# Projections in token order: the residue order made as queries and keys leave PSUM, and for values by a trip through DRAM

## The chip, the cores and the metric

One Trainium2 chip, of which the kernel uses one core. The metric is the device time of one execution in microseconds (us). Five engines matter here: the tensor engine (PE, with its weight loads shown apart as PEld), the vector engine (DVE), the scalar engine (ACT), GpSimd (POOL) and the sync engine (SP), which in this kernel issues every DMA.

## What is computed

The reference is one layer of a decoder trunk on 512 tokens of 1024 channels: a normalisation, one large input projection (`w_in`, 11520 columns), three causal token mixers on slices of it, gates, three branch projections that are merged, and an output projection with a residual. All is float32. Cut to what the change touches:

```python
hn = rms_norm(x, ln_g[l])
proj = jnp.einsum('bsd,dc->bsc', hn, w_in[l])
(qa, ka, va, ga, qb, kb, vb, gb, qc, kc, vc, gc, gate_logits) = jnp.split(proj, ...)
...
DIL_PAIRS = ((128, 1), (512, 4), (2048, 16))      # mixer B: (window, dilation) of three head groups
...
for gi, (w, d) in enumerate(DIL_PAIRS):
    steps = jnp.arange(n_keys[gi]) * d
    idx = t[:, None] + w - steps[None, :]
    k_g = k_pads[gi][:, idx]
    v_g = v_pads[gi][:, idx]
    logits = einsum('bqhd,bqjhd->bhqj', q_c[:, :, gi], k_g) * scale + bias_g[gi][:, None, :]
```

In the groups with dilation 4 and 16 a query sees only keys whose distance is a multiple of 4. Sorted by residue modulo 4, the 512 tokens fall into four tiles of 128, and the queries of a tile have all their keys in the tile of the same residue. That order (residue 0: tokens 0, 4, 8, ..., then residue 1, ...) is called the residue order here.

## The kernel before

Every matrix product is done in three passes, with each float32 operand split in a high and a low part (`whi`, `wlo`, `xhi`, `xlo`; the low part is what the high one leaves over). The normalised hidden state lies transposed in SBUF, as `xhi` and `xlo`, 128 channels by 8 channel tiles by 512 tokens.

The attention work is cut into ten units, in this order: A0, W0, R0, Z0, A1, W1, R1, Z1, C0, C1. The letter is the kind (A is mixer A, W, R and Z are the dilations 1, 4 and 16 of mixer B, C is mixer C), the digit the half of the heads: four heads each. A unit has a projection and an attention:

- Projection (`project`, line 351): for each of four tiles of 128 tokens, 24 matmuls (8 channel tiles by three passes, lines 362 to 364) into one PSUM tile `pj`. The hidden state is the stationary operand (what the weight load brings in, 128 columns), the weight of `w_in` the moving one: 512 columns for queries and keys together, 256 for values. For the units R and Z the stationary operand is `perm_view(xhi[:, k, :], "R")[:, t]`, that is every fourth token: 128 float32 elements that lie 16 bytes apart. For all others it is 128 neighbouring elements.
- Queries and keys leave `pj` by ACT (line 374), are normalised per head (ACT squares, line 376; DVE sums, line 378; POOL takes the power, line 141; DVE multiplies, line 389), are transposed on PE (line 412, the queries reversed within the tile), and are written to SBUF with their gain (units R and Z: ACT, line 415, to `qf` and `kf`). Values leave `pj` by a cast on ACT and a subtraction on DVE (lines 386 and 387, shown as the helpers' lines 130 and 135), to `vhi` and `vlo`.
- Attention of R and Z (`residue_attention`, line 507), for each pair of heads: eight score matmuls (line 522, tile t of queries against tile t of keys), a DVE pass that adds the bias and takes the minimum (436), an exponential on ACT (437), transposes on PE (533), a split of these into `pthi` and `ptlo` (ACT and DVE, 130 and 135), the product with the values (lines 425 to 427, from `mm3`) and an eviction to `oraw` in token order (ACT, line 550). `kf` and `qf` of tile t come from projection tile t alone.

After the unit Z a joint softmax over the three groups follows (lines 711 to 749; its ACT copies `un` stand at line 718). After the units there are the raw gate columns, the gates, the branch products and the output product, all of them runs of matmuls.

Weights of `w_in` are loaded ahead on SP's queue (`load_w`, line 146), into four buffers `w32`, then split by ACT (`whi`, line 130) and DVE or POOL (`wlo`, line 135) into six buffers each. A unit's queries and keys take four of the six, its values two. Line 642 projects queries and keys first, then the values.

The order in which each engine gets its instructions is not the order of the code: the framework schedules the whole program on a timeline of its own, engine by engine, and the queues are then fixed. So PE's queue mixes the attention of one unit with the projection of the next, and each engine works strictly in its queue's order. PSUM has eight banks in four tags of two (`pj`, `tr`, `sc`, `po`).

Of the kernel before, what the change touches and what calls it, by code (L numbers as in the profile page):

```python
# [30 lines left out]
# per unit: steps of the work that fills the tensor engine (the next unit's projections, or raw gate  # L31
# columns) issued before its attention, and their number after each step of the attention
RATION = {"A0": (52, 0.5), "W0": (52, 0.5), "W1": (52, 0.5), "C0": (8, 0.6), "C1": (0, 0.9)}

# kinds of attention: A causal, W window of 128 and itself, C window of 128, R keys 4 apart,
# Z keys 16 apart (as R, three of four masked). Each: length of its row of biases, distance at the
# row's start, distance between neighbours, largest distance.
# [16 lines left out]
# first columns of w_in's parts  # L54
# [37 lines left out]
def perm_view(v, perm):  # L92
    """Last axis of 512 tokens as (tile, ...) in the order of the kind."""
    if perm == "R":
        return v.rearrange("p (i r) -> p r i", r=4)
    return v.rearrange("p (t i) -> p t i", i=128)


def body(tc, x, ln_g, w_in, qk_g, sinks, w_branch, w_out, rel_bias, c_ident, c_onehot, c_mask, c_expand, out):
# [9 lines left out]
    with top:  # L109
# [36 lines left out]
        def load_w(pieces, kts, early=False):  # L146
            """Pieces of one width side by side: source(k0, k1) -> DRAM view [128, k1 - k0, n].
            Returns the high and the low part as functions of the k tile."""
# [29 lines left out]
        def start_x():  # L178
            """Hidden state: normalised, transposed, split."""
# [40 lines left out]
        def start_bias():  # L220
            """Rows of biases by distance, negated, +BIG where the distance is masked; gains, sinks."""
# [39 lines left out]
        def gate_cols(w, c, psum):  # L261
            """psum [128, 512]: columns c .. c+127 of the loaded chunk, on all tokens."""
            whi, wlo = w
            for k in range(KT):
                a = whi(k)[:, c : c + 128]
                T.matmul(psum, a, xhi[:, k, :], start=(k == 0), stop=False)  # L266
                T.matmul(psum, a, xlo[:, k, :], start=False, stop=False)  # L267
                T.matmul(psum, wlo(k)[:, c : c + 128], xhi[:, k, :], start=False, stop=(k == KT - 1))  # L268
                yield
# [37 lines left out]
        with att:  # L307
# [29 lines left out]
            def stack_queries(qn, dst, tsl):  # L337
                """Four heads' queries, each transposed with its high part on rows 0-63 and its low
                part on rows 64-127."""
# [11 lines left out]
            def project(pieces, perm, w, qbuf=None):  # L351
                """Pieces: (type, destination, columns, gain). Types: q, k, v; K and V are the keys
                and values that several query heads share, doubled."""
                whi, wlo = w
                ncol = sum(p[2] for p in pieces)
                for t in range(NT):
                    tsl = slice(t * 128, (t + 1) * 128)
                    pj = ps.tile([128, 512], F32, name="pj", tag="pj")
                    for k in range(KT):
                        xh = perm_view(xhi[:, k, :], perm)[:, t]  # L360
                        xl = perm_view(xlo[:, k, :], perm)[:, t]
                        T.matmul(pj[:, :ncol], xh, whi(k), start=(k == 0), stop=False)  # L362
                        T.matmul(pj[:, :ncol], xh, wlo(k), start=False, stop=False)  # L363
                        T.matmul(pj[:, :ncol], xl, whi(k), start=False, stop=(k == KT - 1))  # L364
                        if k < KT - 1:
                            yield
# [26 lines left out]
                    for ty, dst, m, gc in pieces:  # L393
                        src = pj[:, o : o + m]
                        if ty == "v":
                            split_hi(dst[0][:, t, :m], src)
                            split_lo(dst[1][:, t, :m], src, dst[0][:, t, :m])
# [6 lines left out]
                        else:  # L404
# [9 lines left out]
                            if len(dst) == 1:  # L414
                                A.activation(dst[0][:, :, tsl], tr[:, :npair], AF.Copy, scale=g)
# [23 lines left out]
            def natural_attention(kind, hf, u, stat, oraw):  # L439
                """Queries in token order against the keys from the start (A) or from the tile before."""  # L440
# [66 lines left out]
            def residue_attention(kind, hf, u, stat, oraw):  # L507
                """Tokens in the order of their residues, so that each tile of queries has its keys in
                the tile of the same number."""
                qf, kf, vh, vl = u  # L510
                for p in range(2):
# [6 lines left out]
                    for t in range(NT):  # L518
                        for e in range(2):
                            rows = slice(e * 64, e * 64 + 64)  # L520
                            qs = slice(t * 128, t * 128 + 128)
                            T.matmul(scs[e][:, t], qf[rows, p, qs], kf[rows, p, qs], start=True, stop=True)  # L522
# [30 lines left out]
            def spread(vals, hf, order, use):  # L553
                """vals: for each group [128, NT, 4], factors per (query, head of this half); order:
                the transpose's moving matrix. Calls use(p, g, expanded) with each pair's factors on
                the pair's 128 channels. High and low parts are stacked in one contraction."""
# [40 lines left out]
            def loads(unit, early=False):  # L597
# [10 lines left out]
                return [load_w([win_piece(q + c, 256), win_piece(k + c, 256)], KT, early), load_w([win_piece(v + c, 256)], KT)]  # L608
# [13 lines left out]
            def unit_project(ui, ws):  # L622
                """Queries, keys and values of a unit."""
# [13 lines left out]
                else:  # L637
# [4 lines left out]
                    yield from project([("q", q, 256, gc), ("k", k, 256, gc + 1)], perm, ws[0])  # L642
                    yield from project([("v" if kind in "RZ" else "V", v, 256, 0)], perm, ws[1])
# [6 lines left out]
            for ui, (kind, hf, gi) in enumerate(units):  # L650
# [58 lines left out]
                elif len(bstate["o"]) == 3:  # L709
                    # the groups' maxima and sums to token order, their joint softmax weights  # L710
# [47 lines left out]
        def silu(br):  # L758
            """silu(gate) times the branch, in two parts."""
# [115 lines left out]
```

## Time and profile before

| | |
|---|---|
| median of 3 runs | 892.51 us |
| lowest, highest | 889.96, 894.52 us |
| span of the profiled execution | 891.1 us |
| the profiled execution's own time | not given apart from its span |
| PE busy | 877.7 us (98%), 4295 matmuls |
| PE weight loads busy | 733.4 us (82%) |
| DVE, ACT, POOL busy | 426.1, 413.5, 172.0 us |
| DMA moved | 75.18 MB, mean 84 GB/s |

The busy time of PE is counted from the modelled start to the modelled end of a matmul, and neighbouring matmuls overlap. So 98% doesn't say that PE does all it could: how fast it goes is read from the distance between the starts of two neighbours. The profile's line numbers are those of the kernel above. Where a line is that of a helper (130, 135, 425 to 427), the tile's name says which use it is.

### The profile page before, as it was taken

The numbers are of one execution on the slowest core, as the hardware profiler recorded it, in microseconds if no ns is written. First come the engines' busy times: TensorE is split into PE (matmuls) and PEld (weight loads), VectorE is DVE, ScalarE is ACT, GpSimd is POOL, SyncE is SP. The second block draws the span as 40 slices with busy tenths as digits, with TensorE's granted clock in tenths as the row PEclk, the third lists the DMA queues.
The fourth block names the chain that finished last, engine by engine and source line by source line (L and its number), as shares of the span: only waits on it lengthen the run. The fifth ranks groups of instructions, "written<-read, shape, count | busy, mean of one in ns | idle before, by whom it ended". The sixth has DMA issues, their size and how long they took to land.

```text
span 891.1 us, 11573 instructions
## 1 busy us (share of the span) xinstructions
PE 877.7 (98%) x4295; PEld 733.4 (82%) x4295; DVE 426.1 (48%) x981; ACT 413.5 (46%) x913; POOL 172.0 (19%) x113
## 2 busy tenths in 40 slices
PE   7999999999999999999999999999999999999998
PEld 5888889888978678998899787777888888888886
DVE  6746455344236656434442468554614554322522
ACT  5535553447468546335464585654623432321410
POOL 4333012020112240220210135010402320120100
PEclk9999999999999999999999999999999999999999
DMA  8434113112014221231121132231333232332202
GB/s 264 127 114 133 48 36 97 58 31 76 32 54 119 64 83 55 72 95 37 32 82 47 30 107 58 85 108 48 127 108 96 95 129 84 121 136 75 99 20 95
DMA packets 54077, 75.18 MB, mean 84 GB/s; under 512 B 4451, under 2 KB 36323, under 8 KB 54020
## 3 DMA queue, kind: packets, MB, share of 16 engines
q1 hardware_dynamic: 54020, 74.44, 26.6%
q8 instruction: 34, 0.56, 0.3%
q14 instruction: 23, 0.19, 0.1%
HBM read 70.17 MB, written 4.26 MB: 84 GB/s over the span
## 4 chain that ended last, share of the span: by engine, by line
PE 93%; DVE 2%; ACT 2%; DMA 1%; issue 1%; POOL 0%; SPq 0%; DVEq 0%; POOLq 0%; ACTq 0%
PE pj L362 13%; PE pj L363 13%; PE pj L364 13%; PE pj L266 7%; PE pj L268 7%; PE pj L267 7%; PE acc L834 5%; PE po L499 4%; PE tr L474 3%; PE po L809 3%; PE po L808 3%; PE po L810 2%; PE sc L425 2%; PE sc L522 2%; PE tr L412 1%; PE sc L427 1%
## 5 line engine op out<-in xcount | busy, mean ns | idle before, releaser
L362 PE MATMUL pj<-whi,xhi 128*128 128x512 f32 (+1 forms) x576 | 223.3, 388 | 2.0 <-DVE whi L132 1.4
L363 PE MATMUL pj<-wlo,xhi 128*128 128x512 f32 (+1 forms) x576 | 217.6, 378 | 0.0
L364 PE MATMUL pj<-whi,xlo 128*128 128x512 f32 (+1 forms) x576 | 216.2, 375 | 0.0
L135 DVE TENSOR_TENSOR wlo<-w,whi 128x1024 fp32r<-128x1024 f32 x82 | 110.0, 1351 | 112.9 <-ACT whi L130 112.3
L362 PEld LDWEIGHTS pj<-whi,xhi 128*128 128x128 f32 x576 | 142.5, 247 | 15.8 <-issue 3.0
L363 PEld LDWEIGHTS pj<-wlo,xhi 128*128 128x128 f32 x576 | 143.0, 248 | 10.2 <-issue 1.7
L364 PEld LDWEIGHTS pj<-whi,xlo 128*128 128x128 f32 x576 | 142.7, 248 | 9.0 <-issue 0.5
L130 ACT CAST whi<-w 128x1024 fp32r<-128x1024 f32 x108 | 113.1, 1051 | 62.8 <-PE po L809 31.7
L135 POOL TENSOR_TENSOR wlo<-w,whi 128x1024 fp32r<-128x1024 f32 x28 | 69.0, 2464 | 292.8 <-ACT whi L130 292.8
L141 POOL TENSOR_TENSOR rr<-rv,mhalf 128x8 f32<-128x8 f32 (+2 forms) x40 | 65.7, 1642 | 306.8 <-DVE rv L139 306.6
L266 PE MATMUL pj<-xhi,whi 128*128 128x512 f32 x288 | 114.8, 399 | 0.0
L268 PE MATMUL pj<-xhi,wlo 128*128 128x512 f32 x288 | 113.7, 395 | 0.0
L267 PE MATMUL pj<-xlo,whi 128*128 128x512 f32 x288 | 113.1, 393 | 0.0
L436 DVE CUSTOM_DVE_ANT_0 lg<-sc,bt 128x128 f32<-128x128 f32 (+3 forms) x128 | 42.4, 362 | 79.4 <-PE tr L474 61.6
L268 PEld LDWEIGHTS pj<-xhi,wlo 128*128 128x128 f32 x288 | 54.1, 188 | 11.9 <-issue 0.5
L266 PEld LDWEIGHTS pj<-xhi,whi 128*128 128x128 f32 x288 | 54.3, 188 | 11.6 <-issue 0.2
L267 PEld LDWEIGHTS pj<-xlo,whi 128*128 128x128 f32 x288 | 54.2, 188 | 11.3 <-issue 0.2
L130 ACT CAST pthi<-tr 128x128 fp32r<-128x128 f32 (+3 forms) x112 | 43.7, 400 | 38.6 <-PE tr L474 22.7
L135 DVE TENSOR_TENSOR ptlo<-tr,pthi 128x128 fp32r<-128x128 f32 (+3 forms) x112 | 50.5, 457 | 22.4 <-ACT pthi L130 22.0
L437 ACT ACTIVATE lg<-lg,sm 128x128 f32<-128x128 f32 (+1 forms) x96 | 40.3, 421 | 24.1 <-DVE sm L436 23.8
L378 DVE TENSOR_REDUCE ss<-sq 128x8 f32<-128x512 f32 (+2 forms) x40 | 25.7, 642 | 48.4 <-ACT sq L376 48.1
L800 ACT ACTIVATE gsg<-pj 128x512 f32<-128x512 f32 x24 | 14.3, 596 | 65.9 <-PE pj L268 65.9
(177 smaller groups left out, 1269.4 us busy)
## 6 DMA issues: line engine op xcount, KB each, us to landing
w<-in_w_in SPq DMA_DIRECT2D x54, 512.0 KB, 3.9
w<-in_w_in SPq DMA_DIRECT2D x72, 256.0 KB, 4.2
w<-in_w_branch SPq DMA_DIRECT2D x12, 512.0 KB, 3.2
w<-in_w_out SPq DMA_DIRECT2D x8, 512.0 KB, 4.5
xt<-in_x SPq DMA_DIRECT2D x4, 512.0 KB, 5.4
bt<-scr SPq DMA_DIRECT2D x8, 256.0 KB, 3.6
bt<-scr SPq DMA_DIRECT2D x16, 128.0 KB, 3.3
osp<-oraw SPq DMA_DIRECT2D x4, 512.0 KB, 4.5
```

Of the source, the lines that this page charges most:

```text
L130: A.copy(dst, src)
L135: eng.tensor_tensor(dst, src, hi.bitcast(F32), ALU.subtract)
L141: G.tensor_tensor(r, v, mhalf[:, :n], ALU.pow)
L266: T.matmul(psum, a, xhi[:, k, :], start=(k == 0), stop=False)
L267: T.matmul(psum, a, xlo[:, k, :], start=False, stop=False)
L268: T.matmul(psum, wlo(k)[:, c : c + 128], xhi[:, k, :], start=False, stop=(k == KT - 1))
L362: T.matmul(pj[:, :ncol], xh, whi(k), start=(k == 0), stop=False)
L363: T.matmul(pj[:, :ncol], xh, wlo(k), start=False, stop=False)
L364: T.matmul(pj[:, :ncol], xl, whi(k), start=False, stop=(k == KT - 1))
L436: V.tensor_tensor_reduce(lg, sc, bt, 1.0, init, ALU.add, ALU.min, mcol)
L437: last_exp[0] = A.activation(lg, lg, AF.Exp, bias=mcol, scale=-1.0, accum_out=lcol)
L834: T.matmul(acc[t * 2 + e], part[k // 2][:, k % 2, tsl], wo[q](k)[:, es], start=(k == 0 and q == 0 and part is mhi), stop=(k == KT - 1 and ...
```

## The change

In the projection every unit takes the hidden state in token order. Units R and Z make the residue order afterwards: the copy of queries and keys from PSUM reads its source with a step of four elements and writes 32 neighbours into each of the four residue tiles; values are split into a new tile `vn` (256 high and 256 low columns, in the ring of three buffers `qn`), each token tile is written to a DRAM scratch of 512 rows, and after the fourth two DMAs read it back in residue order into `vhi` and `vlo`. The values of R and Z are now projected before the queries and keys, and their weights are loaded in that order. Because the queries are still reversed in each token tile, the residue tiles of `qf` stand in reverse, and the scores take tile 3 - t of the queries against tile t of the keys.

```diff
@@ def project @@
-                        xh = perm_view(xhi[:, k, :], perm)[:, t]
-                        xl = perm_view(xlo[:, k, :], perm)[:, t]
+                        xh, xl = xhi[:, k, tsl], xlo[:, k, tsl]
...
                         if ty == "v":
-                            split_hi(dst[0][:, t, :m], src)
-                            split_lo(dst[1][:, t, :m], src, dst[0][:, t, :m])
+                            vn = qkv.tile([128, 512], F32R, name="vn", tag="qn", bufs=3)
+                            split_hi(vn[:, :m], src)
+                            split_lo(vn[:, m : 2 * m], src, vn[:, :m])
+                            vscr = dst[2]
+                            nc.sync.dma_start(vscr[tsl, :], vn.bitcast(F32))
+                            if t == NT - 1:
+                                for i in range(2):
+                                    back = vscr[:, i * m : (i + 1) * m].rearrange("(i r) c -> i r c", r=4)
+                                    nc.sync.dma_start(dst[i].bitcast(F32), back)
...
                             if len(dst) == 1:
-                                A.activation(dst[0][:, :, tsl], tr[:, :npair], AF.Copy, scale=g)
+                                src = tr[:, :npair].rearrange("c p (i r) -> c p r i", r=4)
+                                i0 = 32 * t if ty == "k" else 96 - 32 * t
+                                d4 = dst[0].rearrange("c p (r i) -> c p r i", r=4)
+                                A.activation(d4[:, :, :, i0 : i0 + 32], src, AF.Copy, scale=g)
@@ def residue_attention @@
-                            qs = slice(t * 128, t * 128 + 128)
-                            T.matmul(scs[e][:, t], qf[rows, p, qs], kf[rows, p, qs], start=True, stop=True)
+                            qs = slice((3 - t) * 128, (4 - t) * 128)
+                            ks = slice(t * 128, t * 128 + 128)
+                            T.matmul(scs[e][:, t], qf[rows, p, qs], kf[rows, p, ks], start=True, stop=True)
@@ def loads @@
+                if kind in "RZ":
+                    return [load_w(vv, KT), load_w(qk, KT)]
@@ def unit_project @@
+                    if kind in "RZ":
+                        vscr = dp.tile([S, 512], F32, name=f"vscr{ui}")
+                        yield from project([("v", v + (vscr,), 256, 0)], perm, ws[0])
+                        yield from project(pqk, perm, ws[1])
```

The scheduler puts the work of PE and SP in a new order. Three places matter later.

PE's queue before, where the scores of Z0 begin (`sc<-kf,qf`, line 522; the 256-column matmuls in front are the values of Z0, the 512-column ones behind are queries and keys of A1):

```order
L364 MATMUL pj<-whi,xlo 128x256
L522 MATMUL sc<-kf,qf 128x128 x4
L362 MATMUL pj<-whi,xhi 128x512
L363 MATMUL pj<-wlo,xhi 128x512
L364 MATMUL pj<-whi,xlo 128x512
```

So before, all 96 matmuls of A1's queries and keys stand behind the first of these scores.

PE's queue now at the same scores (line 535), the first pair of heads and then the second (line 546 is the transpose of the exponentials; the 256-column matmuls are the values of A1):

```order
L363 MATMUL pj<-whi,xhi 128x512
L364 MATMUL pj<-wlo,xhi 128x512
L535 MATMUL sc<-kf,qf 128x128 x8
L365 MATMUL pj<-whi,xlo 128x512
L363 MATMUL pj<-whi,xhi 128x512
```

```order
L365 MATMUL pj<-whi,xlo 128x256
L546 MATMUL tr<-idr,lg 128x128
L535 MATMUL sc<-kf,qf 128x128 x2
L546 MATMUL tr<-idr,lg 128x128
L535 MATMUL sc<-kf,qf 128x128 x6
L546 MATMUL tr<-idr,lg 128x128 x2
L363 MATMUL pj<-whi,xhi 128x256
```

The scores of Z0 have moved back by 86 of A1's 96 query and key matmuls: 10 of these stand behind them now, then the 96 of A1's values. The same holds of Z1 in front of C0, where 24 query and key matmuls of C0 and the 96 of C1 stand behind the scores.

SP's queue before, around the weights that follow the biases of R0 (`bt`, line 515; `w` is a weight of `w_in`):

```order
L156 DMA w_2271<-in_w_in 128x2x256 x2
L515 DMA bt<-scr 128x128 x5
L156 DMA w_2278<-in_w_in 128x4x256
L156 DMA w_2284<-in_w_in 128x4x256
L156 DMA w_2818<-in_w_in 128x2x256 x2
```

SP's queue now at the same place (`vscr<-vn` writes a tile of Z0's values to DRAM, `vhi<-vscr` and `vlo<-vscr` read all four back):

```order
L401 DMA vscr_1977<-vn 128x512 x2
L156 DMA w_2300<-in_w_in 128x4x256
L401 DMA vscr_1977<-vn 128x512
L156 DMA w_2306<-in_w_in 128x4x256
L405 DMA vhi<-vscr_1977 128x4x256
L526 DMA bt<-scr 128x128 x3
L405 DMA vlo<-vscr_1977 128x4x256
L526 DMA bt<-scr 128x128 x2
L156 DMA w_2840<-in_w_in 128x2x256 x2
```

Six DMAs of values now stand among the biases and the weights of each of the four units R and Z, and those behind a read-back wait on the queue until it may start.

## Rows read from the trace of the kernel before

**Rows 1.** The page's first part: busy time of each engine, its share of the span, instructions.

```profile
PE 877.7 (98%) x4295; PEld 733.4 (82%) x4295; DVE 426.1 (48%) x981; ACT 413.5 (46%) x913; POOL 172.0 (19%) x113
```

**Rows 2.** The page's fourth part: the chain of work that ended last, shares of the span by engine.

```profile
PE 93%; DVE 2%; ACT 2%; DMA 1%; issue 1%; POOL 0%; SPq 0%; DVEq 0%; POOLq 0%; ACTq 0%
```

**Rows 3.** The answer on the tile `pj`: shortest, median and longest weight load in ns, of the unit projections (line 362) and of the raw gate and gate columns (line 266), with first and last start.

```profile
L362 PEld LDWEIGHTS pj<-whi,xhi x576: 186/192/348, 10.7 to 535.1; 128*128 128x128 f32 x192
...
L266 PEld LDWEIGHTS pj<-xhi,whi x288: 186/188/249, 535.5 to 830.0; 128*128 128x128 f32 x144
```

**Rows 4.** The timeline of PE, start and duration in us, in the values of R0, whose stationary operand has the step of four: the first and the last of 11 neighbours, 10 distances.

```profile
148.19 0.40 PE L363 MATMUL pj<-wlo,xhi 128*128 128x256 f32 x1
...
150.54 0.40 PE L364 MATMUL pj<-whi,xlo 128*128 128x256 f32 x1
```

**Rows 5.** The same in the values of A0, whose stationary operand is contiguous: the first and last of 20 neighbours (19 distances), and of a later 21 (20 distances).

```profile
41.75 0.28 PE L362 MATMUL pj<-whi,xhi 128*128 128x256 f32 x1
...
43.91 0.28 PE L363 MATMUL pj<-wlo,xhi 128*128 128x256 f32 x1
...
46.29 0.28 PE L362 MATMUL pj<-whi,xhi 128*128 128x256 f32 x1
...
48.65 0.28 PE L364 MATMUL pj<-whi,xlo 128*128 128x256 f32 x1
```

**Rows 6.** The same for 512 columns: with the step of four in the queries and keys of Z0 (11 neighbours, 10 distances), and contiguous in W0 (15 neighbours, 14 distances).

```profile
168.64 0.40 PE L363 MATMUL pj<-wlo,xhi 128*128 128x512 f32 x1
...
171.02 0.40 PE L364 MATMUL pj<-whi,xlo 128*128 128x512 f32 x1
```

```profile
54.69 0.39 PE L363 MATMUL pj<-wlo,xhi 128*128 128x512 f32 x1
...
57.96 0.39 PE L362 MATMUL pj<-whi,xhi 128*128 128x512 f32 x1
```

**Rows 7.** The timeline of PE where single steps of R0's values alternate with W0's attention.

```profile
166.92 0.28 PE L427 MATMUL sc<-khi,qlo 64*128 64x256 f32 x1
167.12 0.51 PE L362 MATMUL pj<-whi,xhi 128*128 128x256 f32 x1
167.47 0.40 PE L363 MATMUL pj<-wlo,xhi 128*128 128x256 f32 x1
```

**Rows 8.** Windows: busy time of PE, PEld, DVE, ACT and POOL in stretches (instructions in brackets), granted clock, DMA share, GB/s. The first runs from the second scores of Z0 to the end of A1's projection, the second is the same place in the second half (Z1, C0, C1).

```profile
246.00:293.00 47.00, 46.77 (x297) 39.95 (x294) 26.39 (x89) 34.63 (x86) 9.54 (x6) 1.00 0.28 82
...
488.00:536.00 48.00, 46.57 (x298) 39.79 (x295) 28.54 (x106) 35.22 (x92) 10.89 (x7) 1.00 0.24 74
```

**Rows 9.** Groups of ACT instructions in the stretch 246 to 293 us: count, busy us and mean ns of one, then the idle time before them and what ended it.

```profile
L437 ACT ACTIVATE lg<-lg,sm 128x128 f32<-128x128 f32 x16 | 6.2, 389 | 4.4 <-DVE sm L436 4.4
L130 ACT CAST whi<-w 128x1024 fp32r<-128x1024 f32 x6 | 6.1, 1051 | 0.3 <-PE pj L364 0.3
...
L376 ACT ACTIVATE sq<-qn 128x512 f32<-128x512 f32 x4 | 2.5, 634 | 0.1
L374 ACT COPY qn<-pj 128x512 f32<-128x512 f32 x4 | 2.3, 575 | 1.9 <-PE pj L364 1.9
L130 ACT CAST pthi<-tr 128x512 fp32r<-128x512 f32 x4 | 2.1, 589 | 2.6 <-PE tr L533 2.6
```

**Rows 10.** The chain of waits in order of time, start and duration, at the end of Z0's attention.

```profile
269.72 0.24 PE pj L363
271.29 0.62 ACT oraw L550
...
285.73 0.27 ACT vlo L130
286.03 0.30 DVE vlo L135
286.37 0.38 PE pj L362
...
290.10 0.59 PE tr L412 x4
```

**Rows 11.** Groups of the whole run, different shapes apart: what a weight's low part and the copies cost.

```profile
L135 DVE TENSOR_TENSOR wlo<-w,whi 128x1024 fp32r<-128x1024 f32 x82 | 110.0, 1351 | 112.9 <-ACT whi L130 112.3
...
L550 ACT COPY oraw<-po 64x256 f32<-64x256 f32 x32 | 19.7, 615 | 2.2 <-PE po L427 1.8
...
L415 ACT ACTIVATE qf<-tr,gq 128x256 f32<-128x256 f32 x16 | 7.6, 474 | 21.2 <-PE tr L412 21.1
```

**Rows 12.** The page's sixth part: DMA issues by size, median us from issue to landing.

```profile
w<-in_w_in SPq DMA_DIRECT2D x72, 256.0 KB, 4.2
...
bt<-scr SPq DMA_DIRECT2D x16, 128.0 KB, 3.3
osp<-oraw SPq DMA_DIRECT2D x4, 512.0 KB, 4.5
...
oback<-osp SPq DMA_DIRECT2D x4, 512.0 KB, 4.9
```

**Rows 13.** What SP's queue waited for in the whole run: in total us, times, longest.

```profile
SPq L156 <- DVE wlo L135: 286.5, 59, 24.8
```

**Rows 14.** Windows around two drops of the granted clock (the column before the last two).

```profile
201.00:205.00 4.00, 4.00 (x13) 3.21 (x13) 1.54 (x10) 2.86 (x15) 0.00 (x0) 0.57 0.15 29
443.50:447.50 4.00, 4.00 (x13) 3.23 (x12) 1.27 (x9) 2.28 (x12) 0.00 (x0) 0.57 0.20 33
```

More of the change, by code (lines that the diff above doesn't have):

```diff
@@ L607, in loads @@
                     q, k, v = QB + gi * 512, KB + gi * 512, VB + gi * 512
-                return [load_w([win_piece(q + c, 256), win_piece(k + c, 256)], KT, early), load_w([win_piece(v + c, 256)], KT)]
+                qk, vv = [win_piece(q + c, 256), win_piece(k + c, 256)], [win_piece(v + c, 256)]
+                if kind in "RZ":
+                    return [load_w(vv, KT), load_w(qk, KT)]
+                return [load_w(qk, KT, early), load_w(vv, KT)]
             osum = {}
@@ L641, in unit_project @@
                     uq[ui] = q + k + v
-                    yield from project([("q", q, 256, gc), ("k", k, 256, gc + 1)], perm, ws[0])
-                    yield from project([("v" if kind in "RZ" else "V", v, 256, 0)], perm, ws[1])
+                    pqk = [("q", q, 256, gc), ("k", k, 256, gc + 1)]
+                    if kind in "RZ":
+                        vscr = dp.tile([S, 512], F32, name=f"vscr{ui}")
+                        yield from project([("v", v + (vscr,), 256, 0)], perm, ws[0])
+                        yield from project(pqk, perm, ws[1])
+                    else:
+                        yield from project(pqk, perm, ws[0])
+                        yield from project([("V", v, 256, 0)], perm, ws[1])
             def run(gen):
```

## The prediction

> **What bounds the kernel now.** I read the busy table first: PE is busy 98% of the span, no other engine half of it [rows 1], and the chain that ended last lies on PE for 93% [rows 2]. So a shorter stream on PE shortens the run, as long as nothing else becomes late. Next I asked how fast PE goes, by the distance of the starts of neighbours. With a stationary operand of step four, 256-column matmuls start (150.54 - 148.19) / 10 = 0.235 us apart [rows 4]. With a contiguous one it is 2.16 / 19 = 0.114 us, and in a later run 2.36 / 20 = 0.118 [rows 5]. The weight load tells why: in the units it takes 186 to 348 ns, with its median at 192, while in the gate columns, which never have the step, it is 188 [rows 3]. With the step the loads, not the columns, set the pace. At 512 columns the two are nearly equal: 2.38 / 10 = 0.238 with the step, 3.27 / 14 = 0.234 without [rows 6].
>
> Then I looked for a place where PE is not alone. At the end of Z0's attention the chain leaves PE at 269.7 us, runs through ACT, and comes back only at 286.4 [rows 10]. In the stretch 246 to 293 us ACT works 34.6 us of 47 and in its twin of the second half 35.2 of 48 [rows 8]. ACT is near there already.
>
> **The change part by part.**
>
> *Values of R and Z.* 4 units by 4 tiles by 24 make 384 matmuls of 256 columns, which go from 0.235 to 0.114 or 0.118 us: a gain between 44.9 and 46.5 us. I take 45.5. All of it lies on PE, the path.
>
> *Queries and keys of R and Z.* Another 384 of 512 columns at 0.238 - 0.234: 1.5 us.
>
> *Single steps.* Where a projection step alternates with attention, the first matmul after the switch costs 0.35 us with the step [rows 7] in place of 0.235. How often that is saved the rows don't tell; I take 2 us, with ends at 0 and 6.
>
> *Evictions.* The 32 copies to `qf` and `kf` now read PSUM in steps of 16 bytes and take 474 ns before; the nearest row is the copy to `oraw`, as many columns but written with a step, at 615 ns [rows 11]. So 32 x 0.14 = 4.5 us more on ACT, at worst. They stand in the projection phases, where ACT has slack, so I price them at 0, with 4.5 us if the cover is gone. A gain is excluded, as the elements are the same in number.
>
> *The values' split* is the same cast and subtraction as before, into another tile: 0.
>
> *The trip through DRAM.* Per unit four writes of 256 KB and two reads of 512 KB; neighbours in size land in 3.3 to 4.5 us, and the read of the spilled sums in 4.9 [rows 12]. One write and one read after the last tile of values are about 10 us. Behind that tile come 96 query and key matmuls of the same unit, 22 us, before any product with the values can begin. So 0, and if that cover is gone 10 us per unit. On SP's queue the weights behind a read-back wait for it; but SP waits 286 us in the whole run for a free weight buffer [rows 13], so the queue runs well ahead of need. Each weight tile was requested for a buffer that PE had just freed, and the prefetch stays that deep. I price this at 0, too. `vn` shares its ring of three with `qn`, and holds its buffer about 5 us until the write has landed; a tile of values takes PE 2.8 us, three of them 8.4, so the ring suffices.
>
> *What waits newly.* The scores of tile 0 needed projection tile 0; now they need all four, since each tile writes 32 columns into every residue tile. The order shows what the scheduler made of it: Z0's scores have moved behind 86 of A1's 96 query and key matmuls. What is left for PE from there to the end of A1's values is 10 x 0.234 + 96 x 0.118 = 13.7 us of projections and 92 small matmuls. Four transposes take 0.59 us [rows 10], the overlap of the last one included, so I count 0.11 each: 10 us, together 24. ACT has in the same place most of the 34.6 us of [rows 8]: two of the six weight casts at 1.05 and three of the four pairs of copy and square at 0.58 + 0.63 now stand ahead [rows 9], which leaves 34.6 - 2.1 - 3.6 = 29 us, and its waits on DVE and PE (4.4 and 2.6 us) won't all go; I count 2. So ACT needs 31 us where PE needs 24. Of these 7 us some lag into A1's attention, since the two `pj` banks let PE run ahead by a tile; I take 4 for PE. At Z1 and C0 the sums are alike (24 and 96 matmuls, 35.2 us on ACT), another 4. Ends: 0 each, if all of it lags; and 17 each, if ACT keeps its whole idle time of that stretch (47 - 34.6 = 12.4, so 29 + 12.4 - 24).
>
> *The clock.* Twice in R's attention the granted clock is 0.57 over 4 us [rows 14], that is 1.2 GHz instead of 2.4 for most of that time, in stretches of scores and short matmuls. At (1 - 0.57) x 4 it costs 1.7 us each. I leave both in; ends are both gone (-3.4) and two more (+3.4).
>
> *The sum.* 891.1 - 45.5 - 1.5 - 2 + 8 = 850.1 us for the span. The trace's execution has no time apart from its span, and the median of the runs is 1.4 us above that, so **851.5 us** in the median, rounded to 851.
>
> **A rule that speaks against it.** The Trainium skill, in SBUF — State Buffer, section "Door 1: The DMA port swizzle", says that an access pattern in SBUF may step by four float32 for free, as lines are 16 bytes. By that rule a step of four would cost a weight load nothing. The same passage asks for two hits on a line for full speed, and a step of 16 bytes has one; this trace sides with that half, with 0.235 against 0.114 us [rows 3 to 5].
>
> **The rivals.**
>
> 1. *PE alone sets the pace.* The scheduler has filled Z's attention well enough, and ACT's surplus all lags behind into A1's and C0's own attention, where ACT is idle for half the time. For it: PE is hardly idle even now in that stretch, 46.8 of 47 us [rows 8]. Against it: the chain already runs through ACT for 15 us there, with more work on PE beside it [rows 10]. Time: 891.1 - 49 + 1.4 = 843.5 us.
> 2. *The new chains are longer than their cover.* The last query tile, its square, sum, power and transposes, then scores, or the trip of the values, keep PE waiting about 5 us in each of the four units. For it: PE works strictly in order, so a transpose that is late stops the fill behind it. Against: the order puts a tile of projections or more between. Time: 851 + 20 = 871 us.
> 3. *Slower: SP's queue.* The read-back of `vlo` waits until PE has done with the buffer's last user, and the biases and weights behind it stand still. If the weights then come late by a DMA and their split (4.2 us [rows 12], 1.05 [rows 9] and 1.35 [rows 11]) and PE waits for all six tiles of the next unit in turn, that is some 16 us per unit, 64 us in all: 891.1 - 49 + 64 + 1.4 = 907 us. It decides from 12 us per unit on, where it eats the 49. Against it: SP's 286 us of waiting for buffers [rows 13].
> 4. *The change doesn't do what it says.* If the slow pace in R and Z came from something other than the step (from their place beside W's attention, say), the loads would stay slow, and only the 8 us of waits would come: 900 us. Against it: [rows 4] is a stretch of nothing but values. By the sentence on the free step that the Trainium skill has in SBUF — State Buffer, as cited above, this is what would come.
>
> **How the numbers follow.** My forecast has a chance of 0.46, rival 1 0.33, rival 2 0.12, rival 3 0.04, rival 4 0.02; 0.03 is left for waits at their upper ends that add up to no change. The forecast's own range is 845 to 860: from half its waits and two us more of single steps to 8 us of waits at each stage. Down to 838 it takes in rival 1 with the clock drops gone and 2 us more of single steps; up to 872 it takes in rival 2. Outside are rivals 3 and 4, and the upper ends together, some 0.1. A measurement of this kernel can tell a difference from no change from about 0.5% on, 4.5 us. Faster by more than that: 0.46 + 0.33 + 0.12 = 0.91; within it 0.03; slower 0.06.
>
> **What would show it.** The longest weight load in the units' projections falls from 348 to about 190 ns, and 256-column matmuls of R and Z start 0.12 us apart. Their 96 values fill 11 to 12 us of PE where nothing else is mixed in. In the stretch from Z's scores to the end of the following unit's values, the chain of waits lies on ACT, and PE stands idle or waits there for a few us; if it lies on PE throughout, rival 1 holds. The read-backs land before PE's products with the values want them. Wrong would be: idle PE in front of weight loads that wait for `whi` or `wlo` (rival 3), in front of transposes of `qn` or products with `vhi` (rival 2), or loads that still take over 300 ns (rival 4).

## The result, and the profile after

The changed kernel takes 854.2 us in the median (849.95 to 856.25) against 891.8 us of the kernel before on the same chip: a ratio of 0.9565, with a 95% interval of 0.9533 to 0.9597, so 4.4% faster. The forecast was 851 us. The profiled execution has a span of 848.2 us and a time of its own of 849.95.

The busy table of the changed kernel, which answers to [rows 1], and the shares of the chain that ended last, which answer to [rows 2]:

```profile
PE 823.3 (97%) x4295; PEld 664.4 (78%) x4295; DVE 429.1 (51%) x981; ACT 412.8 (49%) x913; POOL 170.1 (20%) x113
...
PE 88%; ACT 5%; DVE 3%; issue 1%; DMA 1%; POOL 1%; DVEq 0%; SPq 0%; POOLq 0%; ACTq 0%
```

PE has 54.4 us less to do, but it idles 848.2 - 823.3 = 24.9 us, where before it idled 891.1 - 877.7 = 13.4. Five points of the chain have gone from PE, three of them to ACT. So a gain of more than 50 us was made, and some 10 of it were given back.

The tile `pj` (shortest, median, longest weight load in ns), which answers to [rows 3], and the timeline of PE in the values of Z0, the first and the last of 11 neighbours, which answers to [rows 4]:

```profile
L363 PEld LDWEIGHTS pj<-whi,xhi x576: 186/188/337, 10.1 to 490.4; 128*128 128x128 f32 x192
```

```profile
169.81 0.28 PE L364 MATMUL pj<-wlo,xhi 128*128 128x256 f32 x1
...
170.98 0.28 PE L365 MATMUL pj<-whi,xlo 128*128 128x256 f32 x1
```

The values of Z0 now start 1.17 / 10 = 0.117 us apart, where R0's were 0.235 before. The median load went from 192 to 188 ns. The longest is still 337 ns. Four loads of 288 to 337 ns stand at the start of the run, from 10 to 14 us, where the clock column says 1.00; 15 of 302 to 329 ns stand at 260 to 263 us, in one of the stretches of the low clock shown next.

Windows of the changed kernel (busy us of PE, PEld, DVE, ACT, POOL, granted clock, DMA share, GB/s): R0's attention and Z0's projection, Z0's attention with the end of Z0's stage, and the same of Z1; then the four drops of the clock, which answer to [rows 14]:

```profile
178.00:240.00 62.00, 62.00 (x341) 50.63 (x340) 32.91 (x89) 38.35 (x95) 16.23 (x9) 1.00 0.31 89
240.00:270.00 30.00, 25.25 (x175) 23.03 (x176) 15.98 (x53) 26.18 (x68) 2.31 (x2) 0.89 0.27 76
...
450.00:510.00 60.00, 54.54 (x329) 43.67 (x328) 39.01 (x138) 41.89 (x113) 19.43 (x13) 0.91 0.22 62
...
246.00:250.00 4.00, 3.88 (x19) 3.27 (x17) 1.66 (x9) 3.96 (x15) 0.00 (x0) 0.57 0.34 115
259.50:263.50 4.00, 4.00 (x21) 4.00 (x22) 1.98 (x6) 3.78 (x7) 1.64 (x1) 0.57 0.21 66
468.00:475.00 7.00, 5.56 (x27) 4.80 (x25) 2.01 (x4) 5.15 (x12) 0.00 (x0) 0.51 0.17 64
502.00:506.00 4.00, 4.00 (x15) 2.62 (x14) 1.98 (x7) 2.16 (x8) 2.55 (x2) 0.57 0.01 3
```

PE never idles from 178 to 240 us. In the two stages of Z it does, 4.75 us of 30 and 5.46 of 60, and in these stretches the clock falls; in the first of them ACT is busy for 26.2 us of 30. The two drops of the kernel before, in R's attention, are gone; four others have come.

The chain of waits at the end of Z0's attention (start, duration), which answers to [rows 10]:

```profile
246.09 1.73 ACT lg L448 x9
247.82 0.50 ACT oraw L563
...
249.58 0.70 DVE ptlo L135
...
255.10 0.61 ACT oraw L563
...
255.72 0.57 ACT un L740
...
256.31 1.05 ACT un L740
...
257.36 1.06 ACT un L740
...
258.46 0.55 PE trb L743 x4
```

This is the picture that was forecast for the stretch: exponentials, copies to `oraw` and `un` on ACT, and PE behind them.

### The profile page after: what moved, and what is told of

Same layout as the page of the kernel before. It is cut to its first block, busy times and chain, and to the rows that moved or that the text cites. A ratio compares the mean times of both kernels' runs of the same rounds, so it can differ in the third digit from the quotient of the medians.

```text
span 848.2 us, 11663 instructions
## 1 busy us (share of the span) xinstructions
PE 823.3 (97%) x4295; PEld 664.4 (78%) x4295; DVE 429.1 (51%) x981; ACT 412.8 (49%) x913; POOL 170.1 (20%) x113
## 4 chain that ended last, share of the span: by engine, by line
PE 88%; ACT 5%; DVE 3%; issue 1%; DMA 1%; POOL 1%; DVEq 0%; SPq 0%; POOLq 0%; ACTq 0%
PE pj L363 12%; PE pj L364 11%; PE pj L365 11%; PE pj L266 8%; PE pj L268 8%; PE pj L267 8%; PE acc L856 5%; PE po L510 4%; PE tr L485 3%; PE po L830 3%; PE po L831 3%; PE po L832 3%; PE sc L436 2%; ACT lg L448 2%; PE tr L420 2%
## 5 line engine op out<-in xcount | busy, mean ns | idle before, releaser
L363 PE MATMUL pj<-whi,xhi 128*128 128x512 f32 (+1 forms) x576 | 204.0, 354 | 1.3 <-ACT xhi L130 0.7
L364 PE MATMUL pj<-wlo,xhi 128*128 128x512 f32 (+1 forms) x576 | 198.0, 344 | 0.0
L365 PE MATMUL pj<-whi,xlo 128*128 128x512 f32 (+1 forms) x576 | 196.6, 341 | 0.0
L363 PEld LDWEIGHTS pj<-whi,xhi 128*128 128x128 f32 x576 | 109.5, 190 | 19.0 <-issue 2.5
L365 PEld LDWEIGHTS pj<-whi,xlo 128*128 128x128 f32 x576 | 109.2, 190 | 13.4 <-issue 1.3
L364 PEld LDWEIGHTS pj<-wlo,xhi 128*128 128x128 f32 x576 | 109.5, 190 | 12.1 <-issue 1.0
L268 PEld LDWEIGHTS pj<-xhi,wlo 128*128 128x128 f32 x288 | 54.4, 189 | 12.0 <-issue 0.5
L448 ACT ACTIVATE lg<-lg,sm 128x128 f32<-128x128 f32 (+1 forms) x96 | 40.2, 420 | 15.4 <-DVE sm L447 15.2
L448 ACT ACTIVATE lg<-lg,sl 128x128 f32<-128x128 f32 (+2 forms) x64 | 33.5, 523 | 26.9 <-DVE sl L447 26.6
```

The costliest lines, as they stand in the source:

```text
L448: last_exp[0] = A.activation(lg, lg, AF.Exp, bias=mcol, scale=-1.0, accum_out=lcol)
```

## The experiments

The times are medians, the intervals those of the ratio to the kernel before. The row after_again is the changed kernel measured once more beside others, with the time it had at first.

| run | us | ratio, 95% interval |
|---|---|---|
| no_reorder | 839.95 | 0.9400, 0.9381 to 0.9420 |
| values_first | 919.87 | 1.0299, 1.0277 to 1.0321 |
| act_relief | 848.99 | 0.9508, 0.9482 to 0.9535 |
| keys_first | 845.30 | 0.9471, 0.9435 to 0.9507 |
| after_again (the changed kernel) | 853.24 | 0.9565, 0.9543 to 0.9587 |
| values_first_fast | 869.07 | 0.9748, 0.9721 to 0.9776 |
| scatter_alone | 840.27 | 0.9419, 0.9406 to 0.9433 |
| keys_first_relief | 850.01 | 0.9533, 0.9516 to 0.9549 |
| no_trip | 864.55 | 0.9697, 0.9668 to 0.9725 |
| trip_alone | 848.12 | 0.9502, 0.9480 to 0.9524 |
| keys_first_r | 836.04 | 0.9374, 0.9351 to 0.9397 |
| before_r | 895.50 | 1.0037, 1.0021 to 1.0053 |

### no_reorder: the step of four alone

On the kernel before:

```diff
-                        xh = perm_view(xhi[:, k, :], perm)[:, t]
-                        xl = perm_view(xlo[:, k, :], perm)[:, t]
+                        xh, xl = xhi[:, k, tsl], xlo[:, k, tsl]
```

> The kernel before, with the stationary operand of R and Z contiguous and nothing else changed; the residue order is left out, so R and Z attend to the wrong neighbours. PE's queue is the same row for row as before. Theory (the step of four is the whole gain, 45.5 + 1.5 + 2 us on PE, and the changed kernel gives about 11 of it back in waits): 843 us, 840 to 846, and ACT-limited stretches as before. Rival (the gain is larger or smaller than the rows of before say, and the waits of the changed kernel are none): 853 to 856, the time of the changed kernel. Rival (the step is not the cause): 892.

839.95 us. Its page, and the windows from Z0's scores to the end of its stage and the same of Z1:

```profile
PE 821.4 (98%) x4295; PEld 661.2 (79%) x4295; DVE 427.0 (51%) x981; ACT 412.3 (49%) x913; POOL 171.5 (20%) x113
```

```profile
236.00:266.00 30.00, 29.76 (x208) 26.71 (x207) 19.03 (x54) 24.77 (x47) 7.91 (x5) 1.00 0.31 89
436.00:496.00 60.00, 58.07 (x362) 48.11 (x361) 39.88 (x142) 41.21 (x110) 17.48 (x12) 1.00 0.26 78
```

The step is the whole gain. The span is 837.2 us, 53.9 less than before; the two clock drops that went with it are worth 2 x 0.43 x 4 = 3.4 of that, which leaves 50.5. And this run is the yardstick for what the changed kernel gives back: 848.2 - 837.2 = 11.0 us of span. PE idles 837.2 - 821.4 = 15.8 us here against 24.9, which is 9.1 of the 11.0, and in the two Z stages alone it is 0.24 + 1.93 against 4.75 + 5.46, that is 8.0.

### values_first: the order alone, with the step

On the kernel before:

```diff
+                if kind in "RZ":
+                    return [load_w(vv, KT), load_w(qk, KT)]
...
+                    if kind in "RZ":
+                        yield from project([("v", v, 256, 0)], perm, ws[0])
+                        yield from project(pqk, perm, ws[1])
```

> The kernel before, with the values of R and Z projected before their queries and keys, the step of four kept and no trip through DRAM. Theory (the scores wait because each token tile writes into all four residue tiles): the order alone costs little, 890 to 895 us. Rival (the scores stand late because the values no longer lie between the queries and keys and the scores, so the next unit's queries and keys are spent first): about 5 us at each Z, 898 to 904 us, though PE has 11 us more of slow values there to hide it.

919.87 us, 27 more than the 893.07 of the kernel before beside it, and outside both expectations. An edit that looked like a mere exchange of two phases costs more than three times the 8 us of waits in the forecast.

### values_first_fast: the order alone, without the step

The same edit on no_reorder.

> The kernel values_first (920 us) with the stationary operand contiguous and nothing else; the residue order is left out, so R and Z attend to the wrong neighbours. PE's queue is that of values_first row for row. No scatter into residue tiles, no trip through DRAM. Theory (the order, values before queries and keys, is what costs the changed kernel its waits): 850 to 858 us, 10 to 18 above no_reorder's 840. Rival (the scatter over all four residue tiles or the trip costs them): 839 to 844. Rival (the order costs the same 27 us with fast loads as with slow ones): 865 to 870.

869.07 us, 29 above no_reorder. So the order costs about the same with fast loads as with slow ones, 29 us against 27: the second rival. Windows of this run just before R0's attention, and in it, and in R1's; behind them the same place of no_reorder:

```profile
170.00:178.00 8.00, 6.01 (x44) 5.24 (x44) 4.07 (x9) 3.70 (x9) 4.04 (x2) 1.00 0.43 132
178.00:192.00 14.00, 13.43 (x65) 11.75 (x63) 6.68 (x40) 8.66 (x35) 0.00 (x0) 0.52 0.08 16
...
407.00:424.00 17.00, 16.24 (x67) 13.64 (x68) 8.12 (x45) 9.98 (x39) 0.00 (x0) 0.51 0.08 14
```

```profile
174.00:182.00 8.00, 8.00 (x40) 5.88 (x38) 3.25 (x11) 4.43 (x13) 3.17 (x2) 1.00 0.25 71
182.00:198.00 16.00, 16.00 (x83) 12.15 (x83) 8.62 (x43) 9.31 (x31) 2.35 (x2) 1.00 0.05 11
```

What stood on PE in the two stretches (group, count, busy us and mean ns, idle), first of values_first_fast from 178 to 192 us, then of no_reorder from 180 to 198:

```profile
L521 PE MATMUL sc<-kf,qf 64*128 64x128 f32 x32 | 6.2, 437 | 0.1
```

```profile
L521 PE MATMUL sc<-kf,qf 64*128 64x128 f32 x32 | 5.7, 304 | 0.0
L362 PE MATMUL pj<-wlo,xhi 128*128 128x512 f32 x13 | 5.3, 410 | 0.0
L363 PE MATMUL pj<-whi,xlo 128*128 128x512 f32 x13 | 5.2, 402 | 0.0
L361 PE MATMUL pj<-whi,xhi 128*128 128x512 f32 x12 | 4.8, 404 | 0.0
```

With the values first, half of Z0's values stand in front of R0's scores in PE's queue, and none of Z0's queries and keys. PE waits 2 us for `qn`, then runs the attention with no 512-column matmul in it, at a clock of 0.52, and the same again in R1. In no_reorder 38 matmuls of 512 columns (12 and twice 13) are mixed into the same attention, and the clock stays at 1.00. The two stretches lose 0.48 x 14 + 0.49 x 17 = 15 us by their clock; that is about the 16.3 us that PE is busy longer here (837.7 against 821.4). Two things differ at once, the 2 us of waiting before and the long matmuls between; no run tells which of them let the clock fall.

The clock is only a little more than half of the cost. The spans are 867.2 and 837.2 us, 30.0 apart, and the other 13.7 us are idle PE. Most of it comes before the scores of R0 and R1. The page of values_first_fast, its window from the last of W0's values to R0's scores with the same of no_reorder behind it, and the longest wait of PE in that window of values_first_fast:

```profile
PE 837.7 (97%) x4295; PEld 674.7 (78%) x4295; DVE 429.9 (50%) x981; ACT 412.9 (48%) x913; POOL 170.5 (20%) x113
```

```profile
99.00:180.00 81.00, 74.30 (x435) 59.30 (x434) 39.19 (x106) 40.57 (x105) 11.76 (x7) 0.99 0.23 68
115.00:182.00 67.00, 66.01 (x369) 52.02 (x368) 38.16 (x100) 38.37 (x99) 13.64 (x8) 1.00 0.25 73
```

```profile
PE tr L411 <- DVE qn L388: 3.6, 2, 2.0
```

PE idles 6.7 us there against 1.0, and about 5 us more than no_reorder once again in front of R1's scores.

### no_trip: the changed kernel without the trip

```diff
-                            vn = qkv.tile([128, 512], F32R, name="vn", tag="qn", bufs=3)
-                            split_hi(vn[:, :m], src)
...
-                                    nc.sync.dma_start(dst[i].bitcast(F32), back)
+                            split_hi(dst[0][:, t, :m], src)
+                            split_lo(dst[1][:, t, :m], src, dst[0][:, t, :m])
```

> The changed kernel without the trip through DRAM: values still first, in token order straight to vhi and vlo, so the products take the values of the wrong tokens; the scatter of queries and keys stays. The scheduler, which no longer sees the trip, puts the work of R's attention as it did in values_first. Theory (the trip is hidden and costs nothing; what counts is the order the scheduler makes, and in values_first it was a bad one): 863 to 870 us, 10 to 16 slower than with the trip. Rival (the trip costs some microseconds in the changed kernel): 846 to 851. Rival (nothing hangs on it): 852 to 855.

864.55 us, 11 slower than with the trip. By way of the scheduler the trip even helps. Without it PE's queue has none of Z0's query and key matmuls in front of R0's scores, and R0's attention runs as in values_first_fast:

```profile
178.00:192.00 14.00, 13.69 (x68) 12.27 (x69) 7.45 (x44) 8.77 (x37) 0.00 (x0) 0.53 0.08 16
```

With the trip the scheduler puts 39 of them in front and 19 more between the two pairs of heads, and the changed kernel has no idle PE and the full clock there. So no_trip differs in the order of PE's queue too, and doesn't by itself price the transfers. The trace of the changed kernel does. Its read-backs of `vlo` for R0 and Z0 are issued at 129.2 and 197.5 us, no landing of the trip that the trace shows takes more than 7.5 us, and the first products with these values start at 201.9 and 243.4 us (the issue for Z0, and the trip's shortest, median and longest landing):

```profile
197.49 0.53 SPq L405 DMA_DIRECT2D vlo<-vscr  x1
...
DMA to landing us min/median/max: 2.0/3.1/7.5
```

### scatter_alone and trip_alone: one at a time, queries and keys first

scatter_alone is the changed kernel with the order of before and without the trip:

```diff
-                if kind in "RZ":
-                    return [load_w(vv, KT), load_w(qk, KT)]
...
+                            split_hi(dst[0][:, t, :m], src)
+                            split_lo(dst[1][:, t, :m], src, dst[0][:, t, :m])
```

trip_alone is the changed kernel with the order of before and without the scatter:

```diff
-                                A.activation(d4[:, :, :, i0 : i0 + 32], src, AF.Copy, scale=g)
+                                A.activation(dst[0][:, :, tsl], tr[:, :npair], AF.Copy, scale=g)
...
-                            qs = slice((3 - t) * 128, (4 - t) * 128)
+                            qs = slice(t * 128, (t + 1) * 128)
```

> The kernel keys_first (845 us) without the trip through DRAM: queries and keys first, in token order with the copy that writes into four residue tiles; the values go straight to vhi and vlo in token order, so the products take the values of the wrong tokens. Theory (what keys_first still has over no_reorder, 5 us, is the scores' wait for four tiles): 844 to 847. Rival (it is the trip): 839 to 841.

> keys_first (845 us) with the plain copy of queries and keys into one tile per projection tile, no scatter; their residue order is left out, so the scores of R and Z are those of other tokens; values take the trip through DRAM. Theory (the scatter is free, scatter_alone 840, and the trip with nothing behind it costs 5 us): 844 to 847. Rival (the two only cost together, since the copies to kf stand behind the copies to oraw on ACT): 839 to 842.

scatter_alone takes 840.27 us, as no_reorder: the scores' wait for all four tiles costs nothing when the values come second. My theory of it falls. trip_alone takes 848.12 us (844.45 to 848.99), a little above what was expected. So with the order of before the trip adds 5 us beside the scatter (keys_first, shown next, against scatter_alone) and 8 without it (trip_alone against no_reorder). These aren't transfers that PE waits for: in keys_first the read-back of R0's `vlo` is issued at 173.6 us, no landing of the trip that the trace shows takes more than 8.7 us, and the first product with these values starts at 197.4. The scheduler lays the queues out anew with the trip, and what PE waits for in R0 is ACT's queue, as the next section shows.

### keys_first and keys_first_r: a better version

keys_first is the changed kernel with the two places of the order as before. keys_first_r adds:

```diff
-                            A.copy(dst[:, jj * 2 : jj * 2 + 2], po[rows, :, e, :])
+                            (V.tensor_copy if kind == "R" else A.copy)(dst[:, jj * 2 : jj * 2 + 2], po[rows, :, e, :])
```

> The changed kernel with queries and keys projected first again, values and their trip through DRAM second. The scores of Z0 then stand behind 20 of A1's 96 query and key matmuls in place of 86. Theory (the place of the scores is what costs the changed kernel its waits): 843 to 849 us. Rival (the trip through DRAM, now without 22 us of matmuls behind it, comes into the path: up to 10 us in each of four units): 856 to 890. Rival (ACT's work sets the pace wherever the scores stand): 852 to 856.

> keys_first with R's copies to oraw on DVE in place of ACT, where the chain of keys_first waited for ACT (qf and kf behind eight copies to oraw, 195 to 210 us and 413 to 427 us). Theory (that queue on ACT is what keys_first still has over scatter_alone): 839 to 842 us. Rival (the copies only move to DVE and the chain with them, as in keys_first_relief): 845 to 850.

keys_first takes 845.30 us, as its theory expected, and 8 less than the changed kernel. What it still waits for is shown by its chain at the end of R0's attention (start, duration):

```profile
201.54 0.51 ACT oraw L563
...
207.49 0.47 ACT qf L426
207.97 0.50 ACT oraw L563
208.47 0.60 ACT oraw L563
209.10 0.48 ACT kf L426
209.63 0.44 PE tr L420 x2
```

`qf` and `kf` of Z0's first tile stand in ACT's queue behind R0's copies to `oraw`, and PE's transposes behind `kf`. From 195 to 210 us ACT is busy for 13.2 us and DVE for 6.2. With these copies on DVE the queue is short: the `kf` copy is done at 205.7 us, and PE idles 834.3 - 818.9 = 15.4 us in the whole run, where keys_first idles 841.3 - 820.9 = 20.4. The kernel takes 836.04 us, 3 less than its theory expected, and less than either kernel of the case; its interval overlaps that of no_reorder. Its chain at the same place:

```profile
202.54 0.59 ACT pthi L130
203.18 0.39 PE po L436
205.23 0.48 ACT kf L426
205.76 0.44 PE tr L420 x2
```

### before_r: is that gain independent of the change?

The same edit on the kernel before.

> The kernel before, step of four and all, with R's copies to oraw on DVE in place of ACT, as in keys_first_r. Theory (those copies stand in front of qf and kf on ACT there too, but PE has slow values beside them, so the queue on ACT costs little while the step is there): 888 to 892 us, 0 to 4 less. Rival (the gain of keys_first_r, 9 us, has nothing to do with the change): 881 to 885.

895.50 us, 0.4% slower than before, and outside both expectations. PE idles 894.7 - 880.8 = 13.9 us there against 13.4, so the move takes no waiting away. But its clock falls where the kernel before has 1.00, and ahead of the first of the moved copies:

```profile
160.00:176.00 16.00, 16.00 (x59) 13.32 (x58) 4.95 (x15) 5.18 (x17) 0.00 (x0) 0.68 0.18 50
```

That is 0.32 x 16 = 5 us, more than the difference. The gain of keys_first_r doesn't carry over to the kernel before; whether it needs the fast loads, the scatter or the trip wasn't tried.

### act_relief and keys_first_relief: less work for ACT in Z

```diff
-                            A.copy(dst[:, jj * 2 : jj * 2 + 2], po[rows, :, e, :])
+                            (V.tensor_copy if kind == "Z" else A.copy)(dst[:, jj * 2 : jj * 2 + 2], po[rows, :, e, :])
...
-                            A.copy(perm_view(un[rows, :], pm), tr[rows])
+                            V.tensor_copy(perm_view(un[rows, :], pm), tr[rows])
```

> The changed kernel, with Z's copies to oraw and the copies un on DVE in place of ACT: in each Z stage 8 x 0.61 and 6 x 0.89, some 10 us, leave ACT. Theory (ACT's own work sets the pace in both Z stages): 4 to 10 us less than the changed kernel, 844 to 850. Rival (it is the length of the chain score, bias, exponential, transpose, split, and the clock that drops in it): 852 to 856, the same.

> keys_first with Z's copies to oraw and the copies un on DVE in place of ACT. Theory (with the scores in front, PE has work beside ACT's and ACT no longer decides): 843 to 847, as keys_first. Rival (ACT still sets the pace at the end of Z's attention): 838 to 842.

act_relief takes 848.99 us, 4 less than after_again and at the low end of what ACT's work was expected to be worth. The chain at the place shown for the changed kernel has only changed its engine:

```profile
255.03 0.62 DVE oraw L563
...
256.36 1.06 DVE un L740
```

So ACT's load is worth some 4 us of the wait. That the length of the chain is the rest is argued from this picture and wasn't tried by itself. keys_first_relief, 850.01 us, missed both expectations: it is 5 us slower than keys_first, though the scores stand in the same places. Its clock is low in three stretches, where keys_first has a single drop in all its units (0.58 from 210 to 214 us):

```profile
263.00:267.00 4.00, 4.00 (x23) 4.00 (x23) 3.43 (x16) 1.36 (x5) 0.00 (x0) 0.57 0.31 68
430.00:434.00 4.00, 3.88 (x18) 3.65 (x19) 1.10 (x3) 2.02 (x6) 0.97 (x1) 0.58 0.08 32
499.00:506.00 7.00, 6.74 (x25) 4.37 (x23) 4.96 (x13) 3.37 (x12) 2.68 (x2) 0.52 0.00 0
```

Which small wait let the clock fall there wasn't tried.

## Why the prediction was right, and where it wasn't

The time was right, 851 against 854.2, but in part by luck. Where the forecast of the span had 891.1 - 49 + 8 = 850.1, the runs show 891.1 - 53.9 + 11.0 = 848.2: the gain and what was given back both came out larger, by 4.9 and 3.0 us, and the two misses partly cancel. In medians no_reorder gains 53 us, and the changed kernel gives 13 to 14 of them back. The cause named for the waits was only half of the cause. The rest of the distance lies around the span: the profiled execution, 849.95 us, was the fastest of the five, and the changed kernel spreads over 6 us, with its four drops of the clock.

- **Values, queries and keys, single steps** (45.5, 1.5 and 2 us). no_reorder shows 53.9 us of span, 50.5 without the clock drops that went with them. The terms hold within 1.5 us together; they weren't measured one by one. Rival 4, another cause than the step, is excluded. The Trainium skill, in SBUF — State Buffer, "Door 1: The DMA port swizzle", lets a step of four float32 pass as free; for a weight load on this chip it is not, by these 50 us.
- **Evictions** (0, at most 4.5 us). The copies take what they took before with a contiguous source, 474 and 471 ns on average against 474 [rows 11], so the upper bound from `oraw` was not needed:

```profile
L426 ACT ACTIVATE qf<-tr,gq 128x256 f32<-128x256 f32 x16 | 7.6, 474 | 21.8 <-PE tr L420 21.7
L426 ACT ACTIVATE kf<-tr,gn 128x256 f32<-128x256 f32 x16 | 7.5, 471 | 0.5 <-PE tr L420 0.4
```

- **The trip** (0). In the changed kernel the transfers are hidden, as the landings under no_trip show. The price without cover, 10 us per unit, was met nowhere: with queries and keys first the trip adds 5 to 8 us in all four units together, and in the place looked at PE waits for a queue and not for a transfer. A write lands after 2.6 us in the median, and SP still waits most for free weight buffers, less than the 286.5 us of [rows 13] but in the same way; what frees them is DVE's `wlo`, not PE, as the prediction has it. PE's own waits name neither `whi` nor `wlo`, so rival 3 is out. Its 16 us per unit didn't follow from its terms either, which make 6.6 us for one tile:

```profile
vscr<-vn SPq DMA_DIRECT2D x16, 256.0 KB, 2.6
```

```profile
SPq L156 <- DVE wlo L135: 238.7, 57, 17.6
```

- **What waits newly** (8 us; this step failed in its reason). The place was right, the end of Z's attention in both halves, with the chain on ACT and PE idle 8.0 us more than in no_reorder. But the step says that the scores move back because each projection tile writes into all four residue tiles. By the order of PE's matmuls in the traces, that dependence alone puts Z0's scores behind 21 of A1's 96 query and key matmuls and costs nothing (scatter_alone). The exchange of values and queries with keys alone puts them behind none (values_first_fast). The two together put them behind 68 (no_trip), and with the trip behind 86. So I had read the new order of PE's queue rightly, and left out one of the two edits that make it: the exchange, which I had priced at nothing and not even listed as an edit of its own. In steps from no_reorder, the scatter adds 0.3 us (scatter_alone), the trip 5.0 (keys_first) and the exchange 7.9 (after_again). The steps depend on their order: by itself, with neither scatter nor trip, the exchange costs 29 us (values_first_fast), most of them before and in R's attention, and with scatter and trip the scheduler finds an order that saves 16 of them (after_again). The chain of [rows 10] leaves PE at 271.1 us, not at 269.7; nothing hangs on that.
- **The clock** (two drops stay, 3.4 us either way). They did not stay. The four new drops lose up to 3 x 0.43 x 4 + 0.49 x 7 = 8.6 us, 5.2 more than before; less in truth, as PE waits in part of them anyway. Of the 11.0 us given back the busy table puts 9.1 down to idle PE and 1.9 to longer work (823.3 against 821.4). A finer division between waiting and the slow clock stays open, since no run has the one without the other.
- **Rival 1**, PE alone at 843.5 us, is refuted for the changed kernel by the chain on ACT and the idle PE; no_reorder and scatter_alone, at 840, come close to it. **Rival 2**, chains longer than their cover, is what values_first_fast shows in front of R's attention, where PE waits for `qn`, and no_trip, too, waits there; the changed kernel escapes most of it.

## What to carry to other kernels

Price every edit of a change by itself, the reordering too: here the order that goes with the trip cost 8 us, while the trip without that order added 5 to 8, and the version with the old order, with the eight copies to `oraw` of each R unit moved to the engine that had room there, is 2% faster than the changed kernel. The prices don't add up, because each edit makes the scheduler lay out the queues anew: the same exchange cost 29 us alone and 8 beside the others. Moving the copies of Z from ACT to DVE only moved the chain; what paid was to move the copies that stood in a queue in front of something that PE waited for.

## What the runs showed of the hardware

The granted clock can carry as much of a cost as idle time, and how much varies: of the 30.0 us that values_first_fast takes over no_reorder 16.3 are longer work and 13.7 idle PE, of the 11.0 of the changed kernel 1.9 and 9.1. In values_first_fast PE counts as busy for 13.43 us of 14 and still runs at 0.52, the level of 1.2 GHz, after it had idled 2 of the 8 us before; the same attention with 512-column matmuls between its short ones runs at 1.00. In before_r the clock is 0.68 over 16 us in which PE counts as busy throughout. A busy share near 100% says nothing on this: the clock column has to be read beside it.
